# Turning v, the gated attention output and q's sums of squares on VectorE with a bounce through DRAM

## The chip, the cores and the metric

The kernel runs on one core of a Trainium2 chip. The metric is the device time in microseconds of one execution. Three executions of the kernel before took 779.36, 779.53 and 779.75 us; the median is 779.53 us. TensorE is called PE in the profile, VectorE DVE, ScalarE ACT, GpSimd POOL; SP is the queue that starts most loads.

## The reference, cut to what matters

The reference is a trunk of two layers over 256 tokens of width 1024. Each layer normalises its input, multiplies it with one wide input matrix, and feeds two branches: a bidirectional chunked gated DeltaNet (branch a, eight heads of 128) and a differential attention (branch b, eight heads). Their gated outputs are projected, merged, projected again and added to the input. The parts that the change touches are these:

```python
qkv = jax.nn.silu(short_conv(jnp.concatenate([q, k, v], axis=-1), conv_w))
q, k, v = jnp.split(qkv, (GDN_QK, 2 * GDN_QK), axis=-1)
q = l2norm(heads(q, GDN_DK))        # x * rsqrt(sum(x*x) + EPS), per token and head
k = l2norm(heads(k, GDN_DK))
v = heads(v, GDN_DV)
...
o = rmsnorm(o, subln_w) * (1.0 - lambda_init)       # branch b
return o * jax.nn.silu(z)                           # then y_b @ w_pb
```

q and k are normalised per token and head; v is only convolved and passed through SiLU. The output of branch b is normalised, gated with silu(z) and projected by w_pb.

## The kernel before, in words

Every float32 projection is made of three products in a rounded format: a high part and a low part of activations and weights are multiplied (high with high, high with low, low with high). A weight block of 256 rows and 512 columns is loaded (line 226, on SP's queue, three buffers), rounded by ScalarE to `hi` (line 230) and completed by VectorE to `lo` (line 232); `hi` and `lo` have two buffers each. The activations are kept transposed, channel by token, in the same two parts.

The order inside a layer is: branch b's values; k's, q's and v's convolutions (`conv`), mixed with the decays, the products of keys and queries, and a triangular inverse by forward substitution on VectorE (`substitute`, lines 670 and 671), whose result goes through DRAM (`udr`) and comes back as T64 and U; the eight attention heads (`head`); the gates z (`z_part`); the merging of the inverses (`merges`); the chunked recurrence (`chunks`: y1p, sp, ks, y2p, qs, po); the output yb of branch b; gate b, projection pb, gate a; branch a's output; the last projection.

`conv` works on channels by tokens, two blocks of 128 channels at a time. The result of one block, 128 channels by 256 tokens, is `f_` (line 536). For k and v the recurrence needs tokens by channels, so TensorE turns four 128x128 squares with the identity into one PSUM bank (line 544). For v, VectorE multiplies the turned bank by the norm of k and writes `vtm` (line 547). For q nothing of the turned bank is kept: ScalarE squares each 128 columns and accumulates the sums into `ssq` (line 556). These are used late, in the factors of branch a (lines 985 to 988).

`gated` (line 950) makes yb and ya: VectorE multiplies four heads of one token tile by the row factor and the gate (line 955), then `split_T` turns the four squares by TensorE (line 189) and writes the high part by ScalarE (line 198) and the low part by VectorE (line 199). yb waits for its row factors `rb`, which POOL makes by a power (lines 136 and 137), and it is read by projection pb (lines 244 to 246). vtm is first read by y1p (line 784).

Which engine does what is written out. The order of each engine's instructions is laid down when the program is built: a planner walks through the program with its own model of times, gives each engine the ready instruction that stands first in the program (some stretches are raised ahead of all others, some instructions are tied behind another one), and assigns buffers. On the chip each engine then takes its instructions in that order and waits at each for what it needs. A DMA that POOL starts stands in POOL's own order, and waits there.

Of the kernel before, what the change touches and what calls it, by code (L numbers as in the profile page):

```python
# [17 lines left out]
P = 128  # L18
# [5 lines left out]
NH = 8  # L24
# [25 lines left out]
def hybrid_encoder(  # L50
# [48 lines left out]
        return ap.unsqueeze(ap.ndim).to_broadcast(list(ap.shape) + [n])  # L99

    mark = {}


    ident = const.tile([P, P], F32, name="ident")
# [28 lines left out]
    def rsqrt_rows(dst, src, scale, n, power=None):  # L133

        pre = small.tile([P, 16], F32, tag="rspre", name="rspre")
        G.tensor_scalar(pre[:, :n], src, scale, EPS, ALU.mult, ALU.add)
        mark["pow"] = G.tensor_tensor(dst, pre[:, :n], (power or mhalf)[:, :n], ALU.pow).ins

    def norm_row(w_row, nm):

# [43 lines left out]
    def split_T(dst, src, m, nm, bank=bank, w=None):  # L184


        pt = bank(f"pt_{nm}{m}")
        for j in range(4):
            tr = T.transpose(pt[:, j * P : (j + 1) * P], src[:, j, :], ident).ins
        mark["turn"] = tr  # L190
        ptv = pt.rearrange("p (j t) -> p j t", j=4)
        hi = dst[:, 0, :, m * P : (m + 1) * P]
        lo = dst[:, 1, :, m * P : (m + 1) * P]
        if w is None:
            a_ = S.copy(hi, ptv).ins
            mark["split"] = a_, V.tensor_tensor(lo, ptv, hi.bitcast(F32), ALU.subtract).ins
        else:
            S.activation(hi, ptv, AF.Copy, scale=w)
            V.scalar_tensor_tensor(lo, ptv, w, hi.bitcast(F32), ALU.mult, ALU.subtract)

    def pair(nm):
        return [big.tile([P, 2, 4, SEQ], F32R, tag="p8", name=f"{nm}_{i}", bufs=4) for i in range(2)]
# [101 lines left out]
        for i in range(2):  # L304
            evac(accs[i], 2 * i)

    blk = lambda b: slice(32 * b, 32 * b + 32)
    halves = (slice(0, 64), slice(64, P))

    def silu2(dst, ps):  # L310
# [30 lines left out]
    for l in range(DEPTH):  # L341
# [174 lines left out]
        def conv(seg, c_base, slot, g):  # L516
            def evac_conv(acc, b0):
                vf = []
                for b in range(2):
                    j4 = b0 + b  # L520
                    cb = c_base // P + 4 * g + j4
                    ca = work.tile([P, SEQ], F32, tag="conv", name=f"cv{seg}{l}{g}{j4}", bufs=2)
                    S.activation(ca, acc[:, b, :], AF.Copy, scale=cw[:, 2, cb : cb + 1])  # L523
                    for j in (0, 1, 3, 4):
                        sft = j - 2
                        o0, o1 = max(0, -sft), SEQ - max(0, sft)
                        V.scalar_tensor_tensor(ca[:, o0:o1], acc[:, b, o0 + sft : o1 + sft],  # L527
                                               cw[:, j, cb : cb + 1], ca[:, o0:o1],
                                               ALU.mult, ALU.add)
# [6 lines left out]
                    mark["conv"] = V.scalar_tensor_tensor(  # L536
                        f_, th.rearrange("p (m t) -> p m t", m=NM), 1.0,
                        ca.rearrange("p (m t) -> p m t", m=NM), ALU.add, ALU.mult).ins
                    vf.append(f_)
                pt = bank_c(f"ct{seg}{l}{g}{b0}")  # L540
                ptv = pt.rearrange("p (b m d) -> p b m d", b=2, m=NM)
                for b in range(2):
                    for m in range(NM):
                        T.transpose(ptv[:, b, m, :], vf[b][:, m, :], ident)
                bs = slice(4 * g + b0, 4 * g + b0 + 2)
                if seg == "v":
                    V.tensor_tensor(vtm[:, :, bs, :].rearrange("p m b d -> p b m d"), ptv,
                                    last(nrm[:, :, bs].rearrange("p m b -> p b m"), P), ALU.mult)
                    return
                if seg == "k":  # L550
                    S.copy(ktm[:, :, bs, :].rearrange("p m b d -> p b m d"), ptv)
                ss = ssk if seg == "k" else ssq
                for b in range(2):
                    for m in range(NM):
                        hd = 4 * g + b0 + b
                        S.activation(sqj[:, :P], ptv[:, b, m, :], AF.Square,
                                     accum_out=ss[:, m, hd : hd + 1])
# [217 lines left out]
        def chunks(g):  # L775
# [47 lines left out]
                V.tensor_tensor(osb(g, c), heads4(po), osb(g, c), ALU.add)  # L823
            yield

        s_all = small.tile([P, NH, 2, NM], F32, tag="s_all", name=f"s_all{l}")
        ssb = small.tile([P, NM, NH], F32, tag="ssb", name=f"ssb{l}")
        ob = e4(f"ob{l}", "eo")
# [121 lines left out]
        def gated(o_, z_, r_, nw_, yT, nm, tiles=range(NM)):  # L950
            for i in range(2):
                for m in tiles:
                    zv, ov = heads4(z_[i][:, m, :]), o_(i, m)
                    for j in range(4):
                        V.scalar_tensor_tensor(ov[:, j, :], ov[:, j, :],
                                               r_[:, m, 4 * i + j : 4 * i + j + 1],
                                               zv[:, j, :], ALU.mult, ALU.mult)
                    split_T(yT[i], ov, m, f"{nm}{i}", w=nw_)
# [119 lines left out]
```

## Time and profile before

| what | us |
|---|---|
| median of three runs | 779.53 |
| span of the profiled execution, first to last instruction | 777.1 |
| PE busy in it | 758.2 |
| DVE busy | 557.3 |
| ACT busy | 474.9 |
| POOL busy | 101.9 |

The profiled execution is told by its span only; its own time outside the span isn't given, and the median of the runs lies 2.4 us above the span. The granted clock of TensorE was 0.996 of full speed over the span. A row of a group gives line, engine, operation, what it writes and reads, shapes and count, then busy time, mean duration in ns, and the idle time of the engine ahead of it with the releaser. A row of the order in time gives start and length in us, then the same names; the square bracket is idle time ahead of it. A row of the chain gives start, length and who the end of the program depended on.

### The profile page before, as it was taken

The numbers are of one execution on the slowest core, as the hardware profiler recorded it, in microseconds if no ns is written. First come the engines' busy times: TensorE is split into PE (matmuls) and PEld (weight loads), VectorE is DVE, ScalarE is ACT, GpSimd is POOL, SyncE is SP. The second block draws the span as 40 slices with busy tenths as digits, with TensorE's granted clock in tenths as the row PEclk, the third lists the DMA queues.
The fourth block names the chain that finished last, engine by engine and source line by source line (L and its number), as shares of the span: only waits on it lengthen the run. The fifth ranks groups of instructions, "written<-read, shape, count | busy, mean of one in ns | idle before, by whom it ended". The sixth has DMA issues, their size and how long they took to land.

```text
span 777.1 us, 13805 instructions
## 1 busy us (share of the span) xinstructions
PE 758.2 (98%) x5222; PEld 647.7 (83%) x5222; DVE 557.3 (72%) x1051; ACT 474.9 (61%) x1042; POOL 101.9 (13%) x137
## 2 busy tenths in 40 slices
PE   8999999999999999999999999999999999999996
PEld 4899879887778888887889888899777788888784
DVE  5686878999974635377677776989999553536782
ACT  5657776557677744564554668655577776356551
POOL 5100461100030100010010025510001110001000
PEclk9999999999999999999999999999999999999998
DMA  7752756554496644346664256755446954343631
GB/s 227 240 177 78 224 146 198 174 172 136 112 207 187 210 135 129 117 144 210 215 224 136 82 160 221 194 170 161 141 137 174 233 164 160 114 133 111 213 110 54
DMA packets 77745, 126.91 MB, mean 163 GB/s; under 512 B 19679, under 2 KB 20015, under 8 KB 77680
## 3 DMA queue, kind: packets, MB, share of 16 engines
q1 hardware_dynamic: 71038, 112.99, 48.4%
q0 software_dynamic: 3936, 9.77, 4.8%
q10 hardware_dynamic: 2706, 3.28, 1.3%
q8 instruction: 41, 0.67, 0.4%
q14 instruction: 24, 0.20, 0.1%
HBM read 121.27 MB, written 4.75 MB: 162 GB/s over the span
## 4 chain that ended last, share of the span: by engine, by line
PE 81%; DVE 7%; DMA 5%; ACT 4%; issue 2%; POOL 0%; SPq 0%; POOLq 0%; ACTq 0%; DVEq 0%
PE pp_vb L282 5%; DMA raw_q<-in_w_in_dram 3%; PE pp_qk L245 2%; PE pp_qk L246 2%; PE pp_qk L244 2%; PE pp_o L282 2%; PE pf_k L298 2%; PE pf_k L302 2%; PE pf_v L298 2%; PE pf_k L300 2%; PE pp_gb L245 2%; PE sc L839 2%; PE pp_gb L244 2%; PE pf_v L302 2%; PE pf_v L300 2%; PE av L865 2%
## 5 line engine op out<-in xcount | busy, mean ns | idle before, releaser
L245 PE MATMUL pp_qk<-lo_qk,hT 128*128 128x512 f32 x128 | 51.3, 401 | 1.0 <-DVE lo_qk L232 1.0
L246 PE MATMUL pp_qk<-hi_qk,hT 128*128 128x512 f32 x128 | 50.1, 391 | 0.0
L230 ACT CAST hi_qk<-raw_qk 128x1024 fp32r<-128x1024 f32 x32 | 33.5, 1046 | 23.6 <-PE pp_qk L246 12.6
L244 PE MATMUL pp_qk<-hi_qk,hT 128*128 128x512 f32 x128 | 46.1, 398 | 0.7 <-ACT hi_qk L230 0.7
L232 DVE TENSOR_TENSOR lo_qk<-raw_qk,hi_qk 128x1024 fp32r<-128x1024 f32 x32 | 40.2, 1257 | 7.6 <-ACT hi_qk L230 7.4
L232 DVE TENSOR_TENSOR lo_pb<-raw_pb,hi_pb 128x1024 fp32r<-128x1024 f32 x16 | 19.6, 1224 | 35.7 <-ACT hi_pb L230 35.7
L298 PE MATMUL pf_q<-hT,hi_q 128*128 128x256 f32 x128 | 36.5, 288 | 0.3 <-ACT hi_q L230 0.2
L298 PE MATMUL pf_v<-hT,hi_v 128*128 128x256 f32 x128 | 36.5, 289 | 0.0
L300 PE MATMUL pf_v<-hT,hi_v 128*128 128x256 f32 x128 | 36.2, 286 | 0.0
L300 PE MATMUL pf_q<-hT,hi_q 128*128 128x256 f32 x128 | 35.9, 284 | 0.0
L848 ACT ACTIVATE es<-sc,mx 128x256 f32<-128x256 f32 x64 | 29.8, 473 | 10.1 <-DVE mx L846 10.0
L298 PE MATMUL pf_k<-hT,hi_k 128*128 128x256 f32 x128 | 35.8, 285 | 0.0
L302 PE MATMUL pf_q<-hT,lo_q 128*128 128x256 f32 x128 | 35.7, 292 | 0.0
L300 PE MATMUL pf_k<-hT,hi_k 128*128 128x256 f32 x128 | 35.7, 283 | 0.0
L232 DVE TENSOR_TENSOR lo_gb<-raw_gb,hi_gb 128x1024 fp32r<-128x1024 f32 x16 | 19.6, 1224 | 22.2 <-ACT hi_gb L230 22.0
L232 DVE TENSOR_TENSOR lo_ga<-raw_ga,hi_ga 128x1024 fp32r<-128x1024 f32 x16 | 19.6, 1226 | 21.0 <-ACT hi_ga L230 21.0
L302 PE MATMUL pf_v<-hT,lo_v 128*128 128x256 f32 x128 | 34.6, 286 | 0.0
L302 PE MATMUL pf_k<-hT,lo_k 128*128 128x256 f32 x128 | 34.4, 285 | 0.0
L230 ACT CAST hi_pb<-raw_pb 128x1024 fp32r<-128x1024 f32 x16 | 16.8, 1049 | 25.1 <-PE pp_pb L246 24.3
L527 DVE SCALAR_TENSOR_TENSOR cvq<-pf_q,cw,cvq 128x254 f32<-128x254 f32 (+1 forms) x64 | 29.7, 476 | 1.8 <-ACT cvq L523 1.4
L527 DVE SCALAR_TENSOR_TENSOR cvv<-pf_v,cw,cvv 128x254 f32<-128x254 f32 (+1 forms) x64 | 30.2, 483 | 0.6 <-ACT cvv L523 0.5
L527 DVE SCALAR_TENSOR_TENSOR cvk<-pf_k,cw,cvk 128x254 f32<-128x254 f32 (+1 forms) x64 | 28.5, 478 | 2.0 <-ACT cvk L523 1.3
(356 smaller groups left out, 2495.5 us busy)
## 6 DMA issues: line engine op xcount, KB each, us to landing
raw_qk<-in_w_in_dram SPq DMA_DIRECT2D x32, 512.0 KB, 3.7
raw_k<-in_w_in_dram SPq DMA_DIRECT2D x16, 512.0 KB, 4.6
raw_q<-in_w_in_dram SPq DMA_DIRECT2D x16, 512.0 KB, 3.7
raw_v<-in_w_in_dram SPq DMA_DIRECT2D x16, 512.0 KB, 3.8
raw_zb<-in_w_in_dram SPq DMA_DIRECT2D x16, 512.0 KB, 3.6
raw_za<-in_w_in_dram SPq DMA_DIRECT2D x16, 512.0 KB, 3.7
raw_gb<-in_w_in_dram SPq DMA_DIRECT2D x16, 512.0 KB, 4.7
raw_o<-in_w_out_dram SPq DMA_DIRECT2D x16, 512.0 KB, 4.5
```

Of the source, the lines that this page charges most:

```text
L230: high = S.copy(hi[:, :, :n], raw[:, :, :n]).ins
L232: mark[nm, kp] = high, V.tensor_tensor(lo[:, :, :n], raw[:, :, :n], hi[:, :, :n].bitcast(F32), ALU.subtract).ins
L244: T.matmul(o, act[kt // 4][:, 0, kt % 4, ts_], hi, start=kt == 0, stop=False)
L245: T.matmul(o, act[kt // 4][:, 0, kt % 4, ts_], lo, start=False, stop=False)
L246: mark["proj"] = T.matmul(o, act[kt // 4][:, 1, kt % 4, ts_], hi, start=False, stop=kt == KT - 1).ins
L282: mark["proj"] = T.matmul(o, a_, w_, start=kt == 0 and a_ is ah and w_ is hi, stop=kt == KT - 1 and a_ is al).ins
L298: T.matmul(o, hi[:, cs], act[kt // 4][:, 0, kt % 4, :], start=first, stop=False, skip_group_check=True)
L300: T.matmul(o, hi[:, cs], act[kt // 4][:, 1, kt % 4, :], start=False, stop=False, skip_group_check=True)
L302: T.matmul(o, lo[:, cs], act[kt // 4][:, 0, kt % 4, :], start=False, stop=done, skip_group_check=True)
L527: V.scalar_tensor_tensor(ca[:, o0:o1], acc[:, b, o0 + sft : o1 + sft], cw[:, j, cb : cb + 1], ca[:, o0:o1], ALU.mult, ALU.add)
L839: mm = T.matmul(sp[n][:, qt * SEQ : (qt + 1) * SEQ], qkT[h // 4][rows, 0, h % 4, qt * P : (qt + 1) * P], qkT[h // 4][rows, 1, h % 4, :], s ...
L848: S.activation(es[:, n, qt, :], spv[:, qt, :], AF.Exp, bias=mx[:, n, qt : qt + 1], accum_out=s_all[:, h, n, qt : qt + 1])
```

## The change

It has three parts, made in both layers.

1. **v.** VectorE turns each of the two blocks of a convolution step in 32x32 squares (`turn_squares`), which leaves the squares of a block in the right orientation but in the wrong partitions. `bounce` puts them in place: POOL stores the tile to DRAM with one DMA, and loads it back with four, one per group of 32 partitions, into `land` (one buffer). POOL then multiplies by the norm of k into `vtm`, in two instructions. TensorE's four turnings and VectorE's product go.
2. **q's sums of squares.** `conv` for q ends with the convolution. After head 5, `key_sums` turns two heads at a time in 32x32 squares, squares them on ScalarE, reduces each square's 32 columns on VectorE, and bounces the partial sums through DRAM; a last reduction adds the four parts into `ssq`. TensorE's turnings and ScalarE's squarings of q go.
3. **yb.** `gated` uses `split_B` in place of `split_T`: VectorE turns squares, the tile bounces through DRAM, ScalarE scales it into a tile of SBUF and rounds it from there, and VectorE subtracts. ya and the merged output keep `split_T`.

The tiles of `squares` have two buffers for all three parts and for the scaled tile of yb. The tile of q's partial sums takes the buffer of the convolution's weight rows (`cwr`).

```diff
+    def turn_squares(tb, src, k0, n):
+        return V.transpose(tb[:, :, k0 : k0 + n, :], src.rearrange("p k (j t) -> p j k t", j=4)).ins
+    def bounce(tb, nm):
+        dd = dram.tile([4, 32, 4, P], F32, tag="bnc", name=f"bnc_{nm}", bufs=4)
+        G.dma_start(out=dd.rearrange("i t j x -> (i t) (j x)"), in_=tb.rearrange("p j k t -> p (j k t)"))
+        land = work.tile([P, 4, 4, 32], F32, tag="land", name=f"land_{nm}", bufs=1)
+        for j in range(4):
+            G.dma_start(out=land[blk(j)].rearrange("t i k d -> t i (k d)"),
+                        in_=dd[:, :, j].rearrange("i t x -> t i x"))
+        return land
+    def squares(nm):
+        return work.tile([P, 4, 4, 32], F32, tag="tb", name=f"tb_{nm}", bufs=2)
+    def split_B(dst, src, m, nm, w):
+        tb = squares(f"{nm}{m}")
+        turn_squares(tb, src, 0, 4)
+        land = bounce(tb, f"{nm}{m}")
+        flat_ = squares(f"w{nm}{m}").rearrange("p a b t -> p a (b t)")
+        S.activation(flat_.rearrange("p k (i t) -> p k i t", i=4), land.rearrange("p i k t -> p k i t"),
+                     AF.Copy, scale=w)
+        hi = dst[:, 0, :, m * P : (m + 1) * P]
+        lo = dst[:, 1, :, m * P : (m + 1) * P]
+        S.copy(hi, flat_)
+        V.tensor_tensor(lo, flat_, hi.bitcast(F32), ALU.subtract)
...
@@ conv
+                tb = squares(f"v{l}{g}{b0}") if slot is None else None
...
+                    if slot is None:
+                        turn_squares(tb, f_, 2 * b, 2)
+                if seg == "q":
+                    return
+                if seg == "v":
+                    land = bounce(tb, f"v{l}{g}{b0}")
+                    for m in range(NM):
+                        G.tensor_tensor(vtm[:, m, bs, :].rearrange("p b (i d) -> p b i d", i=4),
+                                        land[:, :, m::2, :].rearrange("p i b d -> p b i d"),
+                                        last(last(nrm[:, m, bs], 4), 32), ALU.mult)
+                    return
-                if seg == "v":
-                    V.tensor_tensor(vtm[:, :, bs, :].rearrange("p m b d -> p b m d"), ptv,
-                                    last(nrm[:, :, bs].rearrange("p m b -> p b m"), P), ALU.mult)
-                    return
...
+        def key_sums():
+            for h in range(0, NH, 2):
+                tb = squares(f"q{l}{h}")
+                turn_squares(tb, kq[:, h : h + 2, :, 1, :].rearrange("p h m t -> p (h m) t"), 0, 4)
+                S.activation(tb, tb, AF.Square)
+                V.tensor_reduce(qpart[:, :, h : h + 2, :].rearrange("p j h m -> p j (h m)"), tb,
+                                AX.X, ALU.add)
+            G.dma_start(out=qdr.rearrange("i t j x -> (i t) (j x)"),
+                        in_=qpart.rearrange("p j h m -> p (j h m)"))
+            for j in range(4):
+                G.dma_start(out=qsum[blk(j)], in_=qdr[:, :, j].rearrange("i t x -> t i x"))
+            V.tensor_reduce(ssq.rearrange("p m h -> p h m"),
+                            qsum.rearrange("p i (h m) -> p h m i", m=NM), AX.X, ALU.add)
...
         head(5)
+        key_sums()
...
-        gated(lambda i, m: heads4(ob[i][:, m, :]), zb, rb, nw[:, 1:2], ybT, f"yb{l}")
+        gated(lambda i, m: heads4(ob[i][:, m, :]), zb, rb, nw[:, 1:2], ybT, f"yb{l}",
+              split=split_B)
```

More of the change, by code (lines that the diff above doesn't have):

```diff
@@ L101, in hybrid_encoder @@
     mark = {}
+    blk = lambda b: slice(32 * b, 32 * b + 32)
     ident = const.tile([P, P], F32, name="ident")
@@ L305, in proj_fm @@
             evac(accs[i], 2 * i)
-    blk = lambda b: slice(32 * b, 32 * b + 32)
     halves = (slice(0, 64), slice(64, P))
@@ L544, in evac_conv @@
                         T.transpose(ptv[:, b, m, :], vf[b][:, m, :], ident)
[L545 to L552 removed]
+                S.copy(ktm[:, :, bs, :].rearrange("p m b d -> p b m d"), ptv)
                 for b in range(2):
@@ L824, in chunks @@
             yield
+        qdr = dram.tile([4, 32, 4, NH * NM], F32, tag="qdr", name=f"qdr{l}")
+        qss = work.tile([P, 2, 4, NH * NM], F32, tag="cwr", name=f"qss{l}", bufs=1)
+        qpart, qsum = qss[:, 0].rearrange("p j (h m) -> p j h m", m=NM), qss[:, 1]
+        def key_sums():
[11 more added lines that the diff above has]
+                            qsum.rearrange("p i (h m) -> p h m i", m=NM), AX.X, ALU.add)
         s_all = small.tile([P, NH, 2, NM], F32, tag="s_all", name=f"s_all{l}")
@@ L948, in hybrid_encoder, with gated @@
         V.scalar_tensor_tensor(rb, rb, 0.5 * (1.0 - lam0), r0, ALU.mult, ALU.mult)
-        def gated(o_, z_, r_, nw_, yT, nm, tiles=range(NM)):
+        def gated(o_, z_, r_, nw_, yT, nm, tiles=range(NM), split=split_T):
             for i in range(2):
```

5 lines of the change are left out of this document (3 added, 2 removed).

## The prediction

> **What bounds the kernel now.** I read the page first (busy shares, the chain), then TensorE's own waits, then sums by stage, then the groups and the order in time around the three edited places.
>
> ```profile
> span 777.1 us, 13805 instructions
> PE 758.2 (98%) x5222; PEld 647.7 (83%) x5222; DVE 557.3 (72%) x1051; ACT 474.9 (61%) x1042; POOL 101.9 (13%) x137
> PE 81%; DVE 7%; DMA 5%; ACT 4%; issue 2%; POOL 0%; SPq 0%; POOLq 0%; ACTq 0%; DVEq 0%
> ```
>
> TensorE is busy for 98% of the span, and 81% of the chain that ended last is its own work. Its longest wait behind another engine inside the layers is this row, in two occurrences:
>
> ```profile
> PE kk L611 <- DVE A L635: 1.3, 2, 0.8
> ```
>
> So TensorE's queue is nearly solid, and a microsecond of TensorE work taken out is a microsecond gained, unless something else is due at that place. The stages of layer 0 say where that may be (columns: stretch, length, busy time of PE, PEld, DVE, ACT, POOL, then granted clock, DMA share, GB/s):
>
> ```profile
> 96.00:110.00 14.00, 12.23 (x89) 10.81 (x88) 8.59 (x11) 12.80 (x39) 9.04 (x11) 1.00 0.45 147
> ...
> 138.00:216.00 78.00, 77.55 (x431) 63.72 (x431) 76.00 (x175) 49.85 (x113) 3.20 (x1) 1.00 0.51 149
> 216.00:242.00 26.00, 25.81 (x355) 20.51 (x353) 16.91 (x28) 19.32 (x56) 6.18 (x12) 1.00 0.93 211
> 242.00:278.00 36.00, 36.00 (x401) 30.73 (x396) 18.71 (x37) 26.39 (x54) 3.14 (x2) 1.00 0.54 176
> ```
>
> At 96 to 110 us (q's first group, the decays) TensorE is not the bound; at 138 to 216 us (v, the substitution, the first heads) VectorE is as full as TensorE; at 242 to 278 us (yb, gate b) only TensorE is full.
>
> **TensorE's side of the change.** Out go 32 turnings each for q, v and yb over both layers, 96 in all (q's and yb's rows; the turned v has the same shape and count), and nothing comes in.
>
> ```profile
> L544 PE MATMUL ctq<-ident,kq 128*128 128x128 f32 x32 | 6.1, 276 | 0.0
> ```
> ```profile
> L189 PE MATMUL pt_yb<-ident,ob 128*128 128x128 f32 x32 | 5.0, 280 | 0.0
> ```
>
> ```profile
> 268.34 0.87 PE pt_yb L189 x8
> ```
>
> One lasts 0.28 us, but they overlap: on the chain eight take 0.87 us, 0.109 us each. 96 x 0.109 = 10.5 us. The Trainium skill (TensorE: Matmul & The Clock Gate, Part 4: PE-mode transpose) puts a turning at about 275 ns inside a kernel; as an estimate that would be 96 x 0.275 = 26.4 us gained. The trace agrees with that figure as a duration and not as a cost, so 0.109 us stands.
>
> Half of q's turnings (16, the first group of each layer) stand ahead of a place where TensorE waits in any case:
>
> ```profile
> 98.61 1.05 ACT L230 CAST hi_q<-raw_q 128x1024 fp32r<-128x1024 f32 x1 [1.20 <-DMA raw_q<-in_w_in_dram]
> ```
> ```profile
> 104.43 1.16 PE L611 MATMUL kk<-kq 128*128 128x128 f32 x8 [0.48 <-DVE A L635]
> ```
>
> A weight load lands late there, and the products for A wait for the decays. I count these 16 at nothing: 1.7 us lost, 8.7 us left.
>
> **q's sums of squares.** ScalarE loses 32 squarings with their accumulator reads; it gains eight squarings of 512 columns. It is not the bound (61%), so I count that at nothing.
>
> ```profile
> L556 ACT ACTIVATE sqj<-ctq 128x128 f32<-128x128 f32 x32 | 8.9, 278 | 4.7 <-PE ctq L544 4.4
> L556 ACT ACTIVATION_READ_ACCUMULATOR sqj<-ctq 128x1 f32 x32 | 6.5, 202 | 0.0
> ```
>
> VectorE gets, per layer, four turnings and four reductions of 128x512, bounded by the nearest two rows:
>
> ```profile
> L846 DVE TENSOR_REDUCE mx<-sc 128x2 f32<-128x512 f32 x32 | 21.3, 686 | 0.5 <-PE sc L839 0.5
> ```
> ```profile
> L536 DVE SCALAR_TENSOR_TENSOR thv<-thv,cvv 128x256 f32<-128x256 f32 x16 | 6.8, 426 | 0.0
> ```
> ```profile
> L547 DVE TENSOR_TENSOR vtm<-ctv,nrm 128x512 f32<-128x512 f32 x8 | 5.5, 690 | 0.1
> ```
>
> 8 x 0.69 = 5.5 us. They come after head 5, where the stretch 216 to 278 us has 62 us for 35.6 us of VectorE work: nothing, and 5.5 us a layer if that cover were gone. POOL issues five DMAs more there, and q's power (L986) moves behind them; who then stands behind them on POOL is yb's own factor, below. The tile of partial sums shares a buffer with layer 1's row of convolution weights, so that load on SP's queue now waits for the sums; its use lies in the next layer, so it costs nothing.
>
> **v.** VectorE loses four products of 0.69 us a layer and gains eight turnings of 128x256; the nearest row of that size takes 0.43 us: 8 x 0.43 - 4 x 0.69 = +0.7 us. The product goes to POOL, as eight of 128x256 per layer. The only two-input product there now is this one, four of 128x512 in a row, and beside it VectorE is slowed (1.23 us elsewhere for the shape of lo_qk, 0.69 us for dsum):
>
> ```profile
> 106.27 6.45 POOL L795 TENSOR_TENSOR ktm<-ktm,kds 128x512 f32<-128x512 f32 x4 [4.09 <-ACT kds L651]
> ```
> ```profile
> 99.69 1.23 DVE L232 TENSOR_TENSOR lo_q<-raw_q,hi_q 128x1024 fp32r<-128x1024 f32 x1 [0.70 <-ACT hi_q L230]
> ```
> ```profile
> 105.23 0.69 DVE L634 TENSOR_TENSOR dsum<-B 128x512 f32<-128x512 f32 x1 [0.85 <-ACT B L628]
> ...
> 106.63 1.76 DVE L232 TENSOR_TENSOR lo_qk<-raw_qk,hi_qk 128x1024 fp32r<-128x1024 f32 x1
> 108.87 0.97 DVE L634 TENSOR_TENSOR dsum<-B 128x512 f32<-128x512 f32 x1 [0.48 <-issue]
> ```
>
> (1.76 - 1.23) + 0.48 + (0.97 - 0.69) = 1.3 us of VectorE per 6.45 us of POOL. The new products make 8 x 6.45/8 = 6.45 us a layer, so 1.3 us again. VectorE gets 2.0 us a layer where it has 2 us spare of 78; I put half on the path: 2.0 us in all. The bounces themselves are hidden: v's evacuations lie in the stretch that ends at 216 us, the first reader of vtm (y1p) in the one that begins at 242 us, and POOL has a single instruction (3.20 us) in the 78 us before 216. Were the cover gone, y1p would wait for a bounce, some 10 us by the rows under yb.
>
> **yb.** This is the edit with a deadline. Times of layer 0; layer 1 repeats them.
>
> ```profile
> 251.81 0.21 POOL L136 TENSOR_SCALAR rspre<-ssb 128x16 f32<-128x16 f32 x1 [23.83 <-DVE ssb L946]
> 252.11 2.93 POOL L137 TENSOR_TENSOR rb<-rspre,mhalf 128x16 f32<-128x16 f32 x1
> ```
> ```profile
> 256.04 4.29 DVE L955 SCALAR_TENSOR_TENSOR ob<-ob,rb,zb 128x128 f32<-128x128 f32 x16
> ```
> ```profile
> 278.46 0.71 PE L244 MATMUL pp_pb<-hi_pb,ybT 128*128 128x512 f32 x2
> ```
> ```profile
> 285.83 0.62 PE L244 MATMUL pp_pb<-hi_pb,ybT 128*128 128x512 f32 x2
> 286.29 1.05 PE L784 MATMUL ks<-ktm,kq 128*128 128x128 f32 x8
> ```
>
> The 16 gating products run at 256.0 to 260.3 us, the first four being done at 257.1. The projection pb reads the first two turned blocks from 278.46 us and, from its 25th product at 285.83 us, the last two; with 1.7 us of yb's turnings gone ahead of it, the third is due at 284.1 us and the fourth at 284.3. What a bounce costs is bounded by these rows (us from issue to landing, or min/median/max of an issue in ns):
>
> ```profile
> udr<-X POOLq DMA_DIRECT2D x4, 256.0 KB, 4.4
> udr<-lt POOLq DMA_DIRECT2D x4, 256.0 KB, 6.5
> ...
> adr<-A POOLq DMA_DIRECT2D x8, 64.0 KB, 3.7
> la<-adr POOLq DMA_DIRECT2D x2, 256.0 KB, 3.8
> ```
> ```profile
> L656 POOL DMA_DIRECT2D la<-adr x2: 546/548/550, 119.8 to 498.6; - x2
> ```
> ```profile
> L198 ACT ACTIVATE ybT<-pt_yb,nw 128x512 fp32r<-128x512 f32 x8 | 5.4, 701 | 0.0
> ```
> ```profile
> L810 ACT COPY vtm<-y2p 128x512 f32<-128x512 f32 x8 | 4.7, 593 | 1.3 <-PE y2p L784 1.3
> ```
>
> Store 3.7 us; four loads, the last issued 3 x 0.55 us after the first, 1.65 + 3.8 = 5.45 us. The landing tile has one buffer, so the next loads start once ScalarE has read it (0.70 us): a period of 6.15 us. The first block is turned at 257.1 + 0.7 = 257.8 us and lands at 267.0; the others at 273.1, 279.3 and 285.4. Scaling and rounding (0.70 + 0.59 us) make the fourth usable at 286.7 us, 2.4 us late, of which eight products of ks (8 x 0.109 = 0.9 us) can fill a part: TensorE stalls for 1.5 us a layer, 3.0 us in all. I take the adr and la rows because they move 256 KB out and 256 KB back on POOL's queue, as a block does. The ends: no stall, and with the 6.5 us store a fourth block usable at 289.5 us, 5.2 us late, less 0.9: 4.3 us a layer, 8.6 in all. The four more turnings and copies a layer lie in engines that have room. The Trainium skill (DMA: Bandwidth & Descriptors, Anatomy of one DMA) gives 2.0 us plus the bytes at 436 GB/s per DMA, 2.6 us as an estimate for the store; by it no stall is left and the sum would be 3.0 us lower. The rows of this trace lie above it.
>
> **The sum.** -8.7 + 2.0 + 3.0 = -3.7 us on a span of 777.1 us. The median of the runs, 779.5 us, is 2.4 us above this span, which I keep: **775.8 us**.
>
> **Rivals.** First, on the other side: the bounces come later still. The order on each engine is fixed at build time, and ScalarE then waits in line for a landing with the casts of pb's weights and the copies of the state behind it; POOL may also put q's sums ahead of yb's factor. It decides from a delay at which the stall passes (8.7 - 2.0) / 2 = 3.4 us a layer. With the store at 6.5 us and each of the four rounds of loads 1 us longer, the stall is 4.3 + 4 = 8.3 us: 779.5 - 8.7 + 2.0 + 16.6 = **789.4 us**. For it: two DMAs in line per block and one buffer; against: 18 us of gate b in between. Second, the gain ahead of 237 us is given back, because there ScalarE waits for a weight load that TensorE does not set the time of:
>
> ```profile
> 237.40 1.05 ACT L230 CAST hi_gb<-raw_gb 128x1024 fp32r<-128x1024 f32 x1 [1.31 <-DMA raw_gb<-in_w_in_dram]
> ```
>
> Then the 48 counted turnings of q and v, 5.2 us, are lost: **781.0 us**, no change. For it speaks the DMA share of 0.93 there; against, that gate products could be drawn forward. Third, POOL's products stop VectorE for their whole length: 6.45 + 0.7 us a layer in a full stretch: 779.5 - 8.7 + 3.0 + 14.3 = **788.1 us**. The rows above, 1.3 us in 6.45, speak against. The Trainium skill (SBUF — State Buffer, SBUF: two separate sides) has the rule: a GpSimd instruction and a VectorE one with two SBUF inputs exclude each other; the rows agree in part.
>
> **How the numbers follow.** Forecast 0.44; with no stall and no VectorE cost, 770.8 us, 0.04; late bounces 0.30; given back 0.14; VectorE stopped 0.08. The range 769 to 790 us leaves out less than 2 in 10; the forecast's own is 771 to 778. No change is what lies within 0.2%, 1.6 us, about what can be told here: 0.10, all of it from the second rival; the rest of that one, the first and the third make slower 0.42; faster 0.48.
>
> **What would show it.** Right: no row of ctq, ctv or pt_yb, PE's busy time down by some 10 us, and a wait of pp_pb for ybT of one to three us a layer. Wrong: pp_pb or ACT's ybT waiting longer than 3.4 us a layer for the landing tile; lo_qk or the substitution's steps lengthened at 140 to 200 us; a new wait of TensorE near 237 us.

## The result, and the profile after

The changed kernel takes 790.03 us (median of 4 runs, 789.52 to 790.88), the kernel before it beside it 779.44 us: a ratio of 1.0141 with a 95% interval of 1.0129 to 1.0153, so 10 to 12 us slower. The prediction was 775.8 us, faster; even the upper end of its range, 790 us, is just passed.

The page of the changed kernel (span, busy times, shares of the chain that ended last):

```profile
span 788.3 us, 13773 instructions
PE 756.2 (96%) x5126; PEld 640.5 (81%) x5126; DVE 574.8 (73%) x1085; ACT 474.7 (60%) x994; POOL 162.9 (21%) x243
PE 68%; DVE 14%; ACT 6%; DMA 5%; issue 5%; POOL 1%; SPq 0%; POOLq 0%; DVEq 0%; ACTq 0%
```

The 96 turnings are gone from TensorE (5126 products instead of 5222), but its share of the chain fell from 81% to 68%, and VectorE's rose from 7% to 14%. TensorE was idle for 18.9 us of the span before (777.1 - 758.2) and is for 32.1 us now (788.3 - 756.2). The stages of layer 0 say where (stretch, length, busy time of PE, PEld, DVE, ACT, POOL, granted clock, DMA share, GB/s), first of the changed kernel:

```profile
138.00:216.00 78.00, 73.25 (x382) 58.72 (x382) 76.33 (x170) 46.88 (x101) 22.92 (x34) 0.98 0.59 171
```
```profile
242.00:278.00 36.00, 33.84 (x472) 28.64 (x469) 18.55 (x38) 24.96 (x55) 6.54 (x8) 1.00 0.65 205
278.00:343.00 65.00, 62.65 (x377) 54.72 (x376) 37.49 (x68) 39.17 (x88) 11.35 (x18) 1.00 0.43 130
```

and the last of these stretches in the kernel before:

```profile
278.00:343.00 65.00, 65.00 (x384) 57.04 (x383) 34.02 (x62) 33.43 (x78) 3.67 (x4) 1.00 0.42 130
```

At 138 to 216 us TensorE is busy for 73.3 us instead of 77.6, VectorE as full as before, and the granted clock is 0.98. At 278 to 343 us (pb, the chunks, gate a), where nothing but TensorE was full, 2.4 us have opened, and another 2.2 us at 242 to 278 us (36.0 us busy before, 33.8 now). TensorE's waits in the changed kernel (us in total, times, longest):

```profile
PE pp_qk L276 <- DVE lo_qk L263: 2.9, 6, 0.9
PE pp_zb L276 <- DVE lo_zb L263: 2.6, 2, 1.8
PE pp_zb L275 <- DVE cvv L558: 2.4, 2, 1.2
```
```profile
PE pp_pb L275 <- ACT ybT L229: 0.6, 1, 0.6
```

The two rows of zb are new: TensorE waits for VectorE to round zb's weights (lo_zb) and to finish v's convolution (cvv), whose PSUM banks zb's products need. The wait that the prediction looked for, pp_pb for ybT, is only 0.6 us. The new groups on VectorE and POOL cost what was assumed or close to it (the turnings of q, tb_q, take 698 ns each):

```profile
L142 DVE STREAM_TRANSPOSE tb_v<-thv 128x256 f32<-128x256 f32 x16 | 7.0, 436 | 0.0
L872 DVE TENSOR_REDUCE qss<-tb_q 128x16 f32<-128x512 f32 x8 | 5.3, 675 | 0.0
L579 POOL TENSOR_TENSOR vtm<-land_v,nrm 128x256 f32<-128x256 f32 x16 | 13.0, 832 | 25.5 <-DMA land_v<-bnc_v 25.5
```

So the sizes of these steps were right, and the sum was wrong. One thing that differs from the prediction is where the sums of q run: from 182.1 us on, in the stretch where VectorE is full, and not at 216 to 278 us.

```profile
L142 DVE STREAM_TRANSPOSE tb_q<-kq x8: 660/698/706, 182.1 to 576.7; 128x512 f32<-128x512 f32 x8
```

### The profile page after: what moved, and what is told of

It is laid out like the page before. It is cut to its first block, busy times and chain, and to the rows that moved or that the text cites. A ratio compares the mean times of both kernels' runs of the same rounds, so it can differ in the third digit from the quotient of the medians.

```text
span 788.3 us, 13773 instructions
## 1 busy us (share of the span) xinstructions
PE 756.2 (96%) x5126; PEld 640.5 (81%) x5126; DVE 574.8 (73%) x1085; ACT 474.7 (60%) x994; POOL 162.9 (21%) x243
## 4 chain that ended last, share of the span: by engine, by line
PE 68%; DVE 14%; ACT 6%; DMA 5%; issue 5%; POOL 1%; SPq 0%; POOLq 0%; DVEq 0%; ACTq 0%
PE pp_vb L313 5%; PE pp_qk L276 3%; PE pp_qk L277 3%; PE pp_qk L275 2%; PE pp_o L313 2%; PE pp_pa L276 2%; PE pp_pa L275 2%; PE pp_pa L277 2%; DMA bnc_yb<-tb_yb 2%; PE pp_ga L276 2%; PE pp_ga L277 2%; PE pf_v L329 2%; PE pp_za L276 2%; PE pp_ga L275 2%; PE pp_za L277 2%
## 5 line engine op out<-in xcount | busy, mean ns | idle before, releaser
L276 PEld LDWEIGHTS pp_qk<-lo_qk,hT 128*128 128x128 f32 x128 | 24.0, 188 | 10.9 <-DVE lo_qk L263 6.2
L263 DVE TENSOR_TENSOR lo_ga<-raw_ga,hi_ga 128x1024 fp32r<-128x1024 f32 x16 | 19.6, 1226 | 14.5 <-ACT hi_ga L261 14.5
```

The lines of the kernel that those rows point to most:

```text
L263: mark[nm, kp] = high, V.tensor_tensor(lo[:, :, :n], raw[:, :, :n], hi[:, :, :n].bitcast(F32), ALU.subtract).ins
L276: T.matmul(o, act[kt // 4][:, 0, kt % 4, ts_], lo, start=False, stop=False)
```

## The experiments

Differences in us below are the ratio less one times the kernel before (about 779.5 us), with the ends of its 95% interval.

### The three parts alone, and the sums moved

Each part was taken out of the changed kernel by putting the lines of the kernel before in its place.

**q alone**

> Only q's sums of squares by VectorE; v and yb turned by TensorE as before. Theory A (VectorE is the loss: the sums' turnings and reductions, 5.5 us a layer, land in the stretch of 138 to 216 us where VectorE has 2 us to spare): slower than the kernel before by 4 to 7 us, 783 to 787 us. Theory B (the loss is yb's late bounces, and q's sums are hidden, as the prediction counted them): 16 counted turnings of 0.109 us gained, 777.8 us, and never slower. Theory C (POOL's products stopping VectorE): as B.

Measured: 781.88 us, 1.0038 (1.0023 to 1.0053), +3.0 us (1.8 to 4.1). Here the sums run from 89.3 us on, still earlier than in the changed kernel, and TensorE has one large wait that the kernel before has at 1.0 us only:

```profile
PE pp_qk L276 <- DVE lo_qk L263: 7.3, 4, 2.1
```

In layer 0 it ends at 113.2 and 143.2 us. VectorE's reductions of the sums, at 110.1 and 138.6 us, stand ahead of these two lo_qk in its order. As an estimate, 6.3 us more of this wait, less 3.5 us for 32 turnings, is about the loss of q alone; no run takes the wait away.

**v alone**

> Only v by VectorE, the bounce and POOL's product; q and yb as before. Theory A: VectorE gains 0.7 us of its own and about 1.3 us beside POOL a layer in the full stretch, TensorE loses 3.5 us in all: 779 to 782 us. Theory B: 32 turnings of 0.109 us gained, 776 to 778 us. Theory C: 6.5 us a layer of stopped VectorE, 786 to 791 us.

Measured: 785.36 us, 1.0088 (1.0065 to 1.0111), +6.9 us (5.1 to 8.6).

**yb alone**

> Only yb by VectorE and the bounce. Theory A: 3.5 us of turnings gained, the stall for the third and fourth block 1.5 us a layer as the prediction has it or less, because the small products of the chunks are drawn forward: 776 to 779.5 us. Theory B: 4 to 6 us lost a layer, 786 to 790 us. Theory C: as A.

Measured: 784.51 us, 1.0059 (1.0037 to 1.0081), +4.6 us (2.9 to 6.3).

Every part loses by itself, and the three losses, 14.5 us, are more than the loss of the whole. None of the three medians lies in a range that a theory had named for it, so no single theory explains them. The fourth run moved q's sums:

```diff
+            mark["spread"] = V.tensor_copy(lt, X.rearrange("p c i -> p i c")).ins
...
+                with tc.issue_after(mark["spread"]):
+                    turn_squares(tb, kq[:, h : h + 2, :, 1, :].rearrange("p h m t -> p (h m) t"), 0, 4)
```

> The changed kernel with one order added: the four turnings of q's sums may not issue on VectorE before the copy that ends the substitution (at about 221 us), so that they and their reductions fall where VectorE has room. Nothing else is changed. Theory A: 3 to 6 us a layer come back that VectorE lost at 182 to 200 us, 779 to 785 us. Theory B: same as the changed kernel within 2 us, 788 to 792 us, or worse, as the sums' DMAs and q's power move behind or among yb's. Theory C: as B.

Measured: 789.76 us, 1.0143 (1.0122 to 1.0165). The sums did move, to 214.8 us:

```profile
L142 DVE STREAM_TRANSPOSE tb_q<-kq x8: 666/692/711, 214.8 to 601.6; 128x512 f32<-128x512 f32 x8
```

and nothing came back. Theory A falls as far as it named the sums: 5.4 us a layer of VectorE's work out of its full stretch changes nothing here, so the amount of work cannot be all that counts there.

### yb: is it the bounce?

**Without the transfers**

```diff
-        land = bounce(tb, f"{nm}{m}")
+        land = tb
```

> Only yb, with its two transfers left out: ScalarE scales the tile that VectorE has turned, without the bounce, so ybT holds its blocks in the wrong places and the output isn't the reference's. The turning, the extra copy and the order of the program stay. Theory D (what yb's part costs is the bounce: ScalarE's copies of the state stand in line behind the landing, and pb's products come too late to lie between the small products of the chunks): the 3.5 us of turnings are gained and nothing is lost, 775 to 777.5 us. Theory E (the copies and turnings on ScalarE and VectorE or the new order do it, whatever the transfers take): within 2 us of yb alone, 783 to 786 us.

Measured: 775.82 us, 0.9956 (0.9941 to 0.9971), -3.4 us (-4.6 to -2.3). With the transfers left out, the 32 turnings come back at about their price: 32 x 0.109 = 3.5 us. So what yb's part costs, some 8 us (from -3.4 to +4.6), comes with the bounce. How the bounce costs it, POOL's rows of yb alone show, layer 0 (start, duration, x number of issues, and in brackets the idle time before and what ended it):

```profile
262.90 0.66 POOL L147 DMA_DIRECT2D bnc_yb<-tb_yb  x1 [7.33 <-DVE tb_yb L142]
268.44 2.18 POOL L150 DMA_DIRECT2D land_yb<-bnc_yb  x4 [4.88 <-DMA bnc_yb<-tb_yb]
270.61 0.56 POOL L147 DMA_DIRECT2D bnc_yb<-tb_yb  x1
275.46 2.18 POOL L150 DMA_DIRECT2D land_yb<-bnc_yb  x4 [4.29 <-ACT tb_wyb L225]
280.25 0.56 POOL L147 DMA_DIRECT2D bnc_yb<-tb_yb  x1 [2.62 <-DVE tb_yb L142]
284.25 2.17 POOL L150 DMA_DIRECT2D land_yb<-bnc_yb  x4 [3.44 <-DMA bnc_yb<-tb_yb]
291.98 0.56 POOL L147 DMA_DIRECT2D bnc_yb<-tb_yb  x1 [5.56 <-DVE tb_yb L142]
297.30 2.17 POOL L150 DMA_DIRECT2D land_yb<-bnc_yb  x4 [4.75 <-ACT kq L843]
```

Store, loads, store, loads: POOL waits in line for each store to land before it issues that block's loads, and the second store stands behind them. At the third and fourth store POOL itself waits, 2.6 and 5.6 us, for VectorE, which turns these blocks only at 279.3 and 291.0 us. The four stores are 7.7, 9.6 and 11.7 us apart, and the fourth block's loads are issued only at 297 us. In layer 1 the late landing of the first block hits ScalarE, in its rows of the same kernel:

```profile
657.18 0.72 ACT L225 ACTIVATE tb_wyb<-land_yb,nw 128x512 f32<-128x512 f32 x1 [6.00 <-DMA land_yb<-bnc_yb]
657.81 0.56 ACT L822 COPY A<-y1p 128x512 f32<-128x512 f32 x1
```
```profile
PE sp L814 <- ACT A L822: 3.8, 1, 3.8
```

ScalarE stands 6.0 us before a landing, the copy of the state's first factor behind it, and TensorE waits 3.8 us for that copy. Over both layers TensorE waits another 2.5 us for ScalarE's copies `kq` in the chunks (qs and po); the kernel before shows none of these waits.

**Four landing places**

```diff
-        land = bounce(tb, f"{nm}{m}")
+        land = bounce(tb, f"{nm}{m}", src.rearrange("p h e -> p (h e)").rearrange("p (i k t) -> p i k t", i=4, k=4))
```

(and three turned tiles instead of two)

> Only yb, with the same bounce, but each block lands in the place of ob that it was turned from, so there are four landing places instead of one, and three turned tiles instead of two. Theory D1 (the one landing tile and the two turned tiles spread the four bounces over 40 us): the bounces follow each other within some 15 us, and the program comes near the one without transfers, 776 to 780 us, faster than the kernel before or even with it. Theory D2 (the latency of one bounce, with ScalarE's work in line behind it, is enough): 782 to 786 us, as yb alone.

Measured: 784.67 us, 1.0082 (1.0055 to 1.0108). More buffers alone change nothing: the order of the issues on POOL stayed as it was, and the wait of sp for ScalarE is 4.3 us. VectorE's turnings still come one by one, at 260.0, 267.1, 277.1 and last at 288.9 us:

```profile
288.92 0.71 DVE L142 STREAM_TRANSPOSE tb_yb<-ob 128x512 f32<-128x512 f32 x1
```

The three tiles still serve the turned and the scaled blocks alike; whether that or the planner's order puts the last two turnings so late isn't shown.

**Stores first**

```diff
+        late = []
         gated(lambda i, m: heads4(ob[i][:, m, :]), zb, rb, nw[:, 1:2], ybT, f"yb{l}",
-              split=split_B)
+              split=lambda *a, w: late.append(split_B(*a, w=w)))
+        for part in late:
+            next(part)
+        for part in late:
+            next(part, None)
```

(split_B now yields between its store and its loads; the landing in ob's place and the three turned tiles as above)

> Only yb, with the bounce landing in ob's place and three turned tiles, and now all four turnings and stores ahead of the first loads, so that no store stands on POOL's queue behind a wait for another store's landing. Theory D3 (the four bounces in a row on POOL's queue are the loss): the fourth block lands some 15 to 20 us after the first turning instead of 40, and the program is at 775.5 to 779 us. Theory D2 (ScalarE in line behind the first landing): 782 to 786 us.

Measured: 775.64 us, 0.9946 (0.9925 to 0.9967), -4.2 us (-5.8 to -2.6). POOL's rows, layer 0:

```profile
261.64 1.22 POOL L224 DMA_DIRECT2D bnc_yb<-tb_yb  x2 [7.34 <-DVE tb_yb L142]
264.02 0.54 POOL L224 DMA_DIRECT2D bnc_yb<-tb_yb  x1 [1.16 <-DVE tb_yb L142]
267.30 2.74 POOL L228 DMA_DIRECT2D ob<-bnc_yb  x5 [2.74 <-DMA bnc_yb<-tb_yb]
270.03 0.56 POOL L224 DMA_DIRECT2D bnc_yb<-tb_yb  x1
...
275.43 2.72 POOL L228 DMA_DIRECT2D ob<-bnc_yb  x5 [0.92 <-DMA ob<-bnc_yb]
```
```profile
278.00:343.00 65.00, 65.00 (x384) 57.01 (x383) 37.56 (x67) 38.17 (x85) 3.85 (x5) 1.00 0.42 125
```

The last load is issued by 278.2 us instead of 299.5 (yb alone), and TensorE is busy through the whole stretch of 65 us again. Three stores go ahead of the first loads; the fourth follows five of them, as its turning waited for a tile that the first store still read:

```profile
267.11 0.71 DVE L142 STREAM_TRANSPOSE tb_yb<-ob 128x512 f32<-128x512 f32 x1 [1.94 <-DMA bnc_yb<-tb_yb]
```

Against the run with four landing places the edit changes only the order, 784.7 us with the one and 775.6 us with the other, but two things move with it: the stores on POOL, and the turnings on VectorE, the last of them from 288.9 to 267.1 us. Which of the two brings the 9 us wasn't separated. This version beats both kernels.

### v: transfers, products or VectorE?

**Without the transfers** (as above, `land = tb`)

> Only v, with its two transfers left out: POOL's product reads the tile that VectorE has turned, so v's blocks are in the wrong places and the output isn't the reference's. VectorE's turnings and POOL's products stay. Theory F (VectorE's own extra work and POOL's products beside it are what v's part costs, in the stretch where VectorE sets the time): the same as v alone within 2 us, 783.5 to 787.5 us. Theory G (it is the bounce: turned tiles and landing tile are held for the transfers, and v's evacuations wait): 775 to 779 us.

Measured: 784.85 us, 1.0063 (1.0041 to 1.0086), +4.9 us. Most of v's loss stays, so the transfers are not its cause.

**The product by VectorE** (`V.tensor_tensor` for `G.tensor_tensor`)

> Only v, by turning and bounce, but with the product by VectorE instead of POOL: eight products of 128x256 a layer, about 3.4 us more of VectorE and no product on POOL. Theory F1 (the amount of work on VectorE decides): slower than v alone by 4 to 7 us, 789 to 792 us. Theory F2 (POOL's products stop VectorE): VectorE wins back what they took, at least 2 us a layer, against 3.4 us of its own, and the program is within 3 us of v alone or faster, 779 to 787 us. Theory G: VectorE now waits in line for the landing, so slower still, above 792 us.

Measured: 796.93 us, 1.0223 (1.0200 to 1.0247), +17.4 us. It is past theory F1's range and in theory G's: VectorE now stands in line for the landings as well (6.3 us of idle time ahead of the product), and the run does not separate that from the 3.4 us a layer of work.

**VectorE's turnings added to the kernel before**

```diff
+                tb = squares(f"v{l}{g}{b0}") if slot is None else None
...
+                    if slot is None:
+                        turn_squares(tb, f_, 2 * b, 2)
```

> The kernel before, v turned by TensorE as there, and VectorE's eight turnings of 128x256 a layer beside it, read by nobody. TensorE and POOL lose and gain nothing; VectorE gets 8 x 0.436 = 3.5 us a layer in the stretch of 138 to 216 us. Theory F (VectorE sets the time there): 1 us of time or more for each us of VectorE that its 1 to 2 us of spare don't take, 783 to 790 us. Rival (VectorE has room, the loss of v's part is the order or the POOL products): 779.5 to 781 us.

Measured: 787.28 us, 1.0098 (1.0061 to 1.0136), +7.6 us (4.8 to 10.6) for 2 x 3.5 = 7.0 us of VectorE: about paid in full, though the interval is wide. How it is paid isn't what theory F says. TensorE's largest new wait lies far behind v, among the heads at 240 to 245 us and again in layer 1, and there is none for cvv:

```profile
PE av L917 <- ACT aT L913: 6.4, 2, 4.5
```
```profile
242.48 1.04 ACT L261 CAST hi_gb<-raw_gb 128x1024 fp32r<-128x1024 f32 x1 [4.60 <-DMA raw_gb<-in_w_in_dram]
```

The copy aT stands behind this cast on ScalarE, and the cast waits for a weight block of gate b. SP's queue issued that load at 236.8 us instead of 233.1, behind the loads of the substitution's result, whose store on POOL began at 221.7 us instead of 216.7. The granted clock is then 0.59 at 242 to 250 us. So VectorE's added work delays the end of the substitution, and in layer 0 most of the cost comes from there, through SP's queue.

**POOL's products added to the kernel before**

```diff
+                    dum = work.tile([P, 4, 4, 32], F32, tag="land", name=f"dum{l}{g}{b0}", bufs=1)
+                    for m in range(NM):
+                        G.tensor_tensor(dum[:, 2 * m : 2 * m + 2],
+                                        vtm[:, m, bs, :].rearrange("p b (i d) -> p b i d", i=4),
+                                        last(last(nrm[:, m, bs], 4), 32), ALU.mult)
```

> The kernel before with eight two-input products of 128x256 a layer added on POOL, of the shape of those in v's part, each after VectorE's own product for v, read by nobody. Theory F2 (POOL stops VectorE for the whole 6.5 us a layer): 786 us or more. By the rows of the changed kernel (some 1.2 us of longer VectorE steps a layer): 780.5 to 783.5 us. Rival (POOL doesn't matter): 779.5 us within 1 us.

Measured: 781.57 us, 1.0030 (1.0016 to 1.0043), +2.3 us (1.2 to 3.4), for 13.8 us of POOL:

```profile
L581 POOL TENSOR_TENSOR dum<-vtm,nrm 128x256 f32<-128x256 f32 x16 | 13.8, 880 | 88.2 <-DVE cc L905 52.3 <-DVE vtm L577 35.9
```

A sixth of POOL's time, near the fifth that the prediction had read off (1.3 in 6.45), and no stop of the whole length. For v alone that gives an estimate: VectorE's own 1.4 us over both layers, at the full price, and POOL's 2.3 us make 3.7 of 6.9 us, and the 3.5 us of turnings that TensorE saves do not arrive. Where they may go is seen in v alone, layer 0, where VectorE is busy without a gap and TensorE is not (columns as above):

```profile
175.20:177.60 2.40, 0.45 (x4) 0.05 (x2) 2.40 (x5) 0.00 (x0) 1.67 (x2) 1.00 0.40 120
177.60:181.40 3.80, 3.80 (x11) 2.99 (x11) 3.80 (x14) 2.82 (x11) 0.00 (x0) 0.60 0.40 133
```
```profile
177.58 0.50 PE L275 MATMUL pp_zb<-hi_zb,hT 128*128 128x512 f32 x1 [1.95 <-DVE cvv L558]
```

TensorE waits there for v's convolution (3.1 us over both layers), and then runs at a granted clock of 0.60 for 3.8 us. No run takes this wait away, so the rest, some 3 us by these medians, is not settled for v.

### q: why is less work slower?

**Nothing in the place of q's turnings.** Two runs leave the sums out altogether.

> Only q: its turnings and squarings are out and nothing stands in their place; the sums of squares are set to one, so the output isn't the reference's. Theory H (q's turnings lie where TensorE waits for VectorE's lo_qk or for the decays in any case, so all of them gain nothing): 778 to 780 us, and q's part alone at 781.9 us pays 2 to 4 us for the sums. Theory I (16 of 32 counted turnings are gained, as the prediction had it): 776.5 to 778 us, and the sums cost 4 to 5 us.

Measured: 785.21 us, 1.0082 (1.0059 to 1.0106). The fill was issued at the start of the program, with two powers of 2.9 us each that depended on it, ahead of the first norm on POOL, for which TensorE waits 4.5 us; so it was done again in another way.

```diff
-        key_sums()
+        V.tensor_copy(ssq, ssk)
```

> Only q, without turnings, squarings or sums: the sums of squares are copied from those of k by VectorE (0.2 us a layer, after head 5), so the output isn't the reference's. It takes the place of the run that set them to one, whose fill and powers ran on POOL at the start of the program, ahead of the first norm. Theory H (q's turnings gain nothing where they lie): 778.5 to 781 us. Theory I (16 of 32 gained): 776.5 to 778 us.

Measured: 786.94 us, 1.0097 (1.0067 to 1.0127), +7.6 us (5.2 to 9.9). Both theories miss: taking work away from TensorE and ScalarE, and adding next to none, costs more than q's whole part. What changed is the order. The products for A, which stood behind q's first turnings, now start at 86 us instead of 96, but A itself is hardly earlier: VectorE writes its first part at 98.1 us instead of 98.3 and its last at 110.4 instead of 109.9, and the load that brings it back is issued at 118.9 us instead of 119.8. Even so the substitution begins at 132.5 us instead of 137.0, at another place in VectorE's order, and VectorE does more of it early. Which of the steps left out moved it isn't shown. The rows below are the time of the substitution's steps (tile fstmp) on VectorE by stretch; the fourth column is the busy time, of the kernel before and of this one:

```profile
138.00:160.00 22.00, 3.76 (x13) 1.00 0.56 168
160.00:172.00 12.00, 3.04 (x8) 1.00 0.61 175
172.00:186.00 14.00, 3.41 (x9) 1.00 0.41 117
```
```profile
138.00:160.00 22.00, 5.28 (x16) 1.00 0.61 171
160.00:172.00 12.00, 3.27 (x8) 1.00 0.67 186
172.00:186.00 14.00, 4.10 (x10) 0.88 0.30 88
```

12.7 us instead of 10.2 by 186 us, though the first products that read the result (y64p) start at 232.9 us before and at 236.2 us here. That is 2.4 us that VectorE does not give to lo_zb and to v's convolution, and TensorE waits there: `pp_zb <- cvv` is 1.8 us here and not among the waits of the kernel before. q alone, with its sums, has the first step of the substitution at 136.9 us and only 8.9 us of its steps by 186 us; its wait is the one for lo_qk above. The whole change has the first step at 133.1 us, and 10.9 us of steps, so for these two the early substitution is not shown to be the cause.

**The substitution later in the program.** `substitute` and `spread_blocks` were put behind v's first group in the text of the program, in the changed kernel, in the kernel before and in q without sums.

> The changed kernel, with the 31 steps of the substitution and its spreading put behind v's first group in the program's order. Theory J (the substitution, starting some 4 us earlier, stands on VectorE in front of v's convolution and of lo_zb, for which TensorE waits): 3 to 6 us of the loss come back, 784 to 787 us. Theory K (it is the amount of VectorE's work): within 2 us of the changed kernel, 788 to 792 us.

> The control: the kernel before with the same shift of the substitution. Theory J: the substitution is not late there, and the shift brings little, 777 to 780 us, or costs time, as T and U come later, 780 to 785 us. Theory K: as little.

> Only q, without turnings and without sums (copied from k's), at 786.9 us, now with the substitution put behind v's first group. Theory J: 776 to 781 us, 6 us or more come back. Theory K or another order: 785 to 789 us.

Measured: 793.16 us (1.0167, 1.0145 to 1.0190), 780.05 us (1.0008, 0.9999 to 1.0017) and 785.46 us (1.0081, 1.0063 to 1.0098). These don't test the theory: in the first and the last of them the steps up to 175 us stayed within half a microsecond of where they had been on VectorE, so the new place in the text had not reached the order on the engine. The steps themselves had to be tied.

**The substitution held back**

```diff
         conv("v", C_VA, None, 0)
+        c0 = mark["conv"]
         qk_part(1, 0)
         conv("v", C_VA, None, 1)
-        substitute(0, 31)
+        substitute(0, 7)
+        with tc.issue_after(c0):
+            substitute(7, 16)
+        with tc.issue_after(mark["conv"]):
+            substitute(16, 31)
         spread_blocks()
```

> Only q, without turnings and without sums, at 786.9 us, with the steps of the substitution held back on VectorE: step 8 may not issue before the last evacuation of v's first group, step 17 not before that of v's second. Theory J (the substitution ahead of its place takes VectorE from lo_zb and from v's convolution): 5 us or more come back, 777 to 782 us. Theory L (its place is not the cause): 784 to 789 us.

Measured: 774.90 us, 0.9951 (0.9928 to 0.9974), -3.8 us (-5.6 to -2.0): some 11 us less than without the ties. The same rows as above, of this kernel:

```profile
138.00:160.00 22.00, 3.54 (x12) 1.00 0.61 170
160.00:172.00 12.00, 2.47 (x8) 1.00 0.64 176
172.00:186.00 14.00, 3.09 (x8) 1.00 0.46 139
```

The wait for cvv is gone from the list, and the clock stays at 1.00. For q without sums theory J fits, and more comes back than it asked: with the substitution held, the program is faster than the kernel before by about what 32 turnings cost, 3.5 us. What the ties would do to the kernel before, or to q's part with its sums, was not tried, so part of the 3.8 us may be the ties' own.

### yb mended in the whole change

> The whole change, with yb's four turnings and stores ahead of the first loads and the landing in ob's place; q and v as in the changed kernel. Theory D3 (POOL's queue between store and loads is what yb's part lost, 5 us against the kernel before and 9 us against the same part without that loss): the same comes back here, 779 to 785 us, still slower than the kernel before by what q and v cost. Rival (after q's and v's loss the yb chain is covered or not alike, no more than 3 us come back): 787 to 790 us.

Measured: 787.94 us, 1.0084 (1.0055 to 1.0114), with runs from 783.9 to 795.3. Some 4.5 us came back by the ratios, half of what was expected, and the spread is too wide to say more. POOL's rows show that the mending was only half made: the whole change leaves room for two turned tiles, and two stores go ahead of the first loads, three in yb's part alone.

```profile
270.09 1.22 POOL L224 DMA_DIRECT2D bnc_yb<-tb_yb  x2 [7.17 <-DVE tb_yb L142]
276.38 4.37 POOL L228 DMA_DIRECT2D ob<-bnc_yb  x8 [5.08 <-DMA bnc_yb<-tb_yb]
280.75 1.11 POOL L224 DMA_DIRECT2D bnc_yb<-tb_yb  x2
```

## Why the prediction was wrong, step by step

- **The sum, part by part.** Forecast and measured against the kernel before: q -1.7 and +3.0 us, v -1.5 and +6.9, yb -0.5 and +4.6, the whole -3.7 and +11.0. Every part failed, v by most.
- **What bounds the kernel.** Right for the stretches read: TensorE where it was full, VectorE as full at 138 to 216 us. The step that failed is "a microsecond of TensorE work taken out is a microsecond gained" for the 48 turnings of q and v that were counted, 5.2 us: q alone and v alone show nothing of it. TensorE waits there for VectorE instead, for lo_qk in q alone (7.3 us, before 1.0) and for cvv in v alone (3.1 us, before none).
- **A turning at 0.109 us.** Borne out where it could be tested: yb without its transfers gained 3.4 us (2.3 to 4.6) for 32 turnings, yb with its stores first 4.2 us (2.6 to 5.8). At the 0.275 us that the Trainium skill gives for a turning in bf16 (TensorE: Matmul & The Clock Gate, Part 4: PE-mode transpose), 32 turnings would be 8.8 us, an estimate; both intervals lie below it.
- **yb's bounces, +3.0 us.** A stall behind the bounce was right, its size and its path were wrong: the part costs some 8 us beyond its turnings. Two terms failed. The prediction let the first block be turned from 257.1 us and land at 267.0; in yb alone VectorE turns it at 261.9 us, behind all 16 gating products and a step for gate b's weights, and ScalarE reads it at 274.4 us. "A period of 6.15 us" held the loads and ScalarE's read, but neither the next store nor VectorE's late turnings; the measured steps are 7.7, 9.6 and 11.7 us. And TensorE did not stall at pp_pb, but behind ScalarE's copies of the state, as the first rival had it, though with another cause. That its 789.4 us meets the measured time is luck: it wanted 16.6 us of stall, and TensorE's waits in the chunks and at pb sum to 4.6 us in the changed kernel; the rest is what q and v lost.
- **q's sums at nothing "after head 5".** They did not run there: in q alone they run from 89.3 us on and stand ahead of lo_qk, in the changed kernel from 182.1 us on. Yet in the changed kernel moving them there brought nothing, so that term isn't the whole of q's loss. The turnings themselves were priced by what they cost, and not by the order that they kept: with nothing put in their place the program is 7.6 us slower, and with the substitution held as well it is 3.8 us faster. By which step the turnings had kept the substitution in its place stays open.
- **v, +2.0 us.** POOL's part was sized right (2.3 us measured over both layers; 2.6 us read from the rows), VectorE's 0.7 us a layer too. "Half on the path" was wrong: VectorE's turnings, added alone, were about paid in full, 7.6 us for 7.0, though by a path through SP's queue that v alone doesn't show. With the turnings' lost gain that leaves some 3 us of v's 6.9 that no run has named.
- **The other rivals.** The second had a right idea, that the gain is given back, but mostly in the wrong place: TensorE's new waits are at zb, 5.0 us in all. At raw_gb ScalarE waits 2.0 us in layer 0, before 1.3, and TensorE 0.8 us for the copy aT behind it. The third falls with POOL's products added: 2.3 us in all, where it wanted 6.45 us a layer.
- **What would show it.** "lo_qk or the substitution's steps lengthened at 140 to 200 us" pointed the right way: single substitution steps last up to 0.80 us in the changed kernel, before 0.44; the stated wait of pp_pb did not come, as the chunks' products had been drawn forward into its place (po at 309.8 to 322.5 us, before 318.3 to 331.7).

## What to carry to other kernels

A sum of durations holds only while the order on the engines stays: when a step is removed, ask what stood behind it, when that will now run, and which full engine it will then take time from. Where blocks pass through DRAM on one queue, count a store, its loads and the step that makes the next block in one line, and put the stores ahead of the first load that waits for one. A transfer's cost is tested most cheaply by leaving it out and keeping the rest.

## What the hardware showed that was not expected

After a wait, TensorE ran at half clock for 2.7 us. In the changed kernel, layer 0, VectorE's late lo_zb leaves TensorE 1.1 us of work in 2.5 us; work resumes at 183.9 us, and from 185.4 us on the granted clock is 0.50:

```profile
181.00:183.50 2.50, 1.07 (x8) 0.63 (x6) 2.50 (x6) 0.74 (x3) 1.52 (x3) 1.00 0.07 25
185.40:188.10 2.70, 2.70 (x8) 2.08 (x7) 2.56 (x6) 0.69 (x1) 1.05 (x2) 0.50 0.78 225
```

The wait of 1.8 us thus cost 1.4 us more, and the one in v alone 1.5 us (3.8 us at 0.60). It doesn't always: in q alone a similar one left TensorE 1.1 us of work in 3.2 us, and the clock stayed.

```profile
110.00:113.20 3.20, 1.08 (x9) 0.64 (x7) 3.20 (x6) 0.78 (x1) 3.20 (x4) 1.00 0.01 2
113.20:118.00 4.80, 4.80 (x21) 3.95 (x22) 4.60 (x6) 1.73 (x3) 1.49 (x3) 1.00 0.88 207
```

The Trainium skill (TensorE: Matmul & The Clock Gate, Part 1: The HAM clock gate) tells of a gate that looks at a free-running window of 3.4 us and halves the clock after an idle one. A window that runs free may be why one wait is followed by half clock and the other not; no run shows the window. In one point the trace differs from that rule: in the 3.4 us ahead of 185.4 us TensorE was without work for 1.8 us only, and the clock fell all the same.
